# Dilated attention in a two-stream encoder: both heads of a pair side by side, queries and keys stored block by block

## Chip, core and metric

The kernel runs on one core of a Trainium2 chip. The metric is the device time of one execution in microseconds. The five engines that the text names are PE (TensorE, with PEld for its weight loads), DVE (VectorE), ACT (ScalarE), POOL (GpSimd) and SP (which issues transfers).

## What is computed

Two independent sequences ("streams") of 512 tokens and width 1024 pass through a trunk of two layers with shared weights. Layer 0 mixes tokens by dilated window attention and a Hyena convolution, layer 1 by a bidirectional RWKV recurrence; each is followed by a convolutional feed-forward part. The change is in the attention of layer 0. There are three groups of four heads of width 64, with (window, dilation) = (128, 1), (512, 4), (2048, 16):

```python
s = jnp.einsum('bnqhd,bnkhd->bhnqk', qc, kw) * (Dh ** -0.5)   # q, k: the tokens of one residue class
s = jnp.where(valid, s + alibi, NEG_INF)                      # alibi: -slope * |distance|
m = jnp.max(s, axis=-1, keepdims=True)
p = jnp.exp(s - m)
den = jnp.sum(p, axis=-1, keepdims=True)
o = jnp.einsum('bnhqk,bnkhd->bnqhd', p / den, vw)
```

The outputs of the three groups are then merged per head, weighted by their denominators.

## The kernel before

Activations lie transposed, channels on the partitions and 512 tokens in the free dimension. A dense product (`dense`, L124) loads a weight tile (tile `wraw`, a transfer issued by ACT), splits it into a high part on ACT (`whi`, L108) and a low part on POOL (`wlo`, L112), and makes 24 matmuls of FP32R into a PSUM tile `pd`, of which there are three. An evacuation function then copies `pd` out.

Work is written as Python generators that yield their estimated cost. `weave` (L84) and `run` (L1283) interleave them by these estimates, and a scheduler under the program then sets each engine's order. In the first stage the attention of stream 0 is interleaved with `ada_params` (L192), which streams 48 weight tiles `adaw` of 1 MB through three buffers and multiplies each in four matmuls of 32 columns. Stream 1's attention runs later, between the feed-forward matmuls of stream 0.

The attention (L447) goes through six parts (g, hp): group g of three, head pair hp of two. While one part attends, the next is projected. A projection makes `V` (the value columns of the group's four heads, for hp = 0; PSUM tiles `pv`) and two tiles `qk0` and `qk1` of 128 x 512: queries and keys of the two heads of the pair, one head in each half of the partitions (rows 0 to 63 and 64 to 127). In groups 1 and 2 the 512 tokens are four blocks of 128 tokens with equal index modulo 4. `perm(ap, g, b)` picks block b with a stride of four tokens; for V it is applied to the stationary operand.

`attend` (L484) takes one head of the pair after the other. For group 0 each of four blocks has its own score tile of 256 or 384 keys. For groups 1 and 2 the four blocks of 128 queries by 128 keys share one score tile. DVE adds the masked ALiBi term into an SBUF tile `sb` and takes the maximum into `nm` (L503, L504, L514, L516). `attend_blocks` (L525) makes the exponential on ACT (L527), transposes on PE (`self.tr`), copies the result into `pt` on ACT or DVE (L536, L534), and multiplies it with `V` into the half of the partitions of the tile `ops` that belongs to the head. All score tiles, transpositions, `ops` and the accumulator of `ada_params` are PSUM tiles `ps` from one pool of five buffers per stream (L671). At the end ACT copies `ops` to `O`, reordering the tokens of groups 1 and 2 (L521).

After both streams' attention, `combine` (L545) multiplies in the merging weights; its matmuls with `e` (tiles `cme`) have 64 columns and alternate between the halves of the partitions of their output. In the RWKV loop, the matmuls of `X` with `AR` (lines 1193 to 1195) alternate in the same way between the halves of their input partitions.

Of the kernel before, what the change touches and what calls it, by code (L numbers as in the profile page):

```python
# [17 lines left out]
L = 512  # L18
# [33 lines left out]
class K:  # L52
# [387 lines left out]
    def attention(self, s, hs, ap, op, then, early):  # L440
# [11 lines left out]
        def project(g, hp):  # L452
# [18 lines left out]
            for i, m in enumerate((g * 2 + hp, 6 + g * 2 + hp)):  # L471
                t = ap.tile([128, L], F32, tag=f"qk{i}", bufs=2, name=f"qk{i}")
                qk[g, hp].append(t)
                yield from self.dense(a["win"][m], KC, xs, lambda ps: nc.scalar.activation(t, ps, AF.Copy, scale=0.125 if i == 0 else 1.0))

        parts = [(g, hp) for g in range(3) for hp in range(2)]
        yield from project(*parts[0])
# [7 lines left out]
    def attend(self, ap, g, hp, qk, V, rel, nm, den, O, op):  # L485
        nc = self.nc
        ops = self.ps()
        last = None
        for h in range(2):
            row = slice(h * 64, h * 64 + 64)  # L490
            head = hp * 2 + h
            slope = -(2.0 ** (-8.0 * (g * 4 + head + 1) / 12))
            q, k = (t[row] for t in qk)
            blocks = []
            if g == 0:
                for b in range(4):
                    k0, k1 = max(0, b - 1), min(3, b + 1) + 1
                    w = (k1 - k0) * 128
                    ps = self.ps()
                    self.mm(ps[:, :w], q[:, b * 128:b * 128 + 128], k[:, k0 * 128:k1 * 128], start=True, stop=True)  # L500
                    sb = ap.tile([128, 512], F32, tag="sb", bufs=3, name="sb")
                    o = 128 if b == 0 else 0
                    nc.vector.scalar_tensor_tensor(sb[:, :w], rel[:, o:o + w], slope, ps[:, :w], ALU.mult, ALU.add)  # L503
                    nc.vector.tensor_reduce(nm[:, g, b, head:head + 1], sb[:, :w], AX.X, ALU.max, negate=True)  # L504
                    blocks = [(b, sb[:, :w], [(kb, (kb - k0) * 128) for kb in range(k0, k1)])]
                    last = self.attend_blocks(ap, g, head, row, blocks, V, nm, den, ops, last)
                    yield 860 + 600
            else:
                ps = self.ps()
                for b in range(4):  # L510
                    self.mm(ps[:, b * 128:b * 128 + 128], self.perm(q, g, b), self.perm(k, g, b), start=True, stop=True)
                sb = ap.tile([128, 512], F32, tag="sb", bufs=3, name="sb")
                s3 = sb.rearrange("p (b k) -> p b k", b=4)
                nc.vector.scalar_tensor_tensor(s3, rel[:, None, 256 + 128 * g:384 + 128 * g].to_broadcast([128, 4, 128]), slope,  # L514
                                               ps.rearrange("p (b k) -> p b k", b=4), ALU.mult, ALU.add)
                nc.vector.tensor_reduce(nm[:, g, :, head], s3, AX.X, ALU.max, negate=True)  # L516
                blocks = [(b, s3[:, b], [(b, 0)]) for b in range(4)]
                last = self.attend_blocks(ap, g, head, row, blocks, V, nm, den, ops, last)
                yield 4 * (218 + 110 + 218)
        t = op.tile([128, L], F32, tag=f"O{g}{hp}", name="O")  # L520
        nc.scalar.copy(self.unperm(t, g), self.unperm_src(ops, g))  # L521
        O[g, hp] = t

    def attend_blocks(self, ap, g, head, row, blocks, V, nm, den, ops, last):
        nc = self.nc  # L525
        for b, p, keys in blocks:
            nc.scalar.activation(p, p, AF.Exp, bias=nm[:, g, b, head:head + 1], accum_out=den[:, g, b, head:head + 1])  # L527
            tp = self.ps()
            w = len(keys) * 128
            for kb, o in keys:  # L530
                self.tr(tp[:, o:o + 128], p[:, o:o + 128], self.ident)
            pt = ap.tile([128, 384], F32, tag="pt", bufs=2, name="pt")
            if b % 2:
                nc.vector.tensor_copy(pt[:, :w], tp[:, :w])  # L534
            else:
                nc.scalar.copy(pt[:, :w], tp[:, :w])  # L536
            for n, (kb, o) in enumerate(keys):
                mm = self.mm(ops[row, b * 128:b * 128 + 128], V[:, kb, head * 64:head * 64 + 64], pt[:, o:o + 128],
                                      start=n == 0, stop=n == len(keys) - 1)
                if n == 0 and last is not None:  # L540
                    self.after(mm, last)
            last = mm
        return last

    def combine(self, s, ap, nd, z, O, out):  # L545

# [36 lines left out]
    def hyena_in(self, s, hs, pool, tmp):  # L583
# [5 lines left out]
        for part, c in ((1, 0), (1, 1), (2, 0), (2, 1), (0, 0), (0, 1)):  # L589
            i = part * 2 + c  # L590

            def evac(ps):
                if part == 2:
                    t = tmp.tile([128, L], F32, tag="sb", bufs=3, name="hv")
                else:
                    t = (x0 if part == 0 else z)[c]
                self.dwconv(t, ps, lambda j: self.v("sw", j * 6 + i), self.v("sb", i))
                if part == 2:
                    nc.gpsimd.tensor_tensor(z[c], z[c], t, ALU.mult)
# [885 lines left out]
```

## Time and profile before

| | us |
|---|---|
| median of the three runs shown | 3595.82 (3590.41 to 3604.41) |
| the profiled execution | 3581.8 |
| its span, first to last instruction | 3580.0 |
| PE busy | 3311.5 (92%) |
| DVE, ACT, POOL busy | 1707.0, 1576.7, 1603.4 |
| first scores of stream 0 / last products of stream 0 begin | 133.04 / about 377 |
| first scores / last products of stream 1 | about 501 / about 849 |

A row of the timeline has the start, the time from the first start to the last end, the engine, the line, the operation, the tiles (written<-read), for PE the part of the array (rows*columns) and the shape of the output, and xN for N records merged. Helper functions record the matmuls, so all of them stand on L78 and all transpositions on L81; they are told apart by their tiles. In brackets stands the idle time of the engine ahead, and what ended it.

### The profile page before, as it was taken

The numbers are of one execution on the slowest core, as the hardware profiler recorded it, in microseconds if no ns is written. First come the engines' busy times: TensorE is split into PE (matmuls) and PEld (weight loads), VectorE is DVE, ScalarE is ACT, GpSimd is POOL, SyncE is SP. The second block draws the span as 40 slices with busy tenths as digits, with TensorE's granted clock in tenths as the row PEclk, the third lists the DMA queues.
The fourth block names the chain that finished last, engine by engine and source line by source line (L and its number), as shares of the span: only waits on it lengthen the run. The fifth ranks groups of instructions, "written<-read, shape, count | busy, mean of one in ns | idle before, by whom it ended". The sixth has DMA issues, their size and how long they took to land. (4 is left out here: it accounts for less than half of the span.)

```text
span 3580.0 us, 62660 instructions
## 1 busy us (share of the span) xinstructions
PE 3311.5 (92%) x24082; PEld 2367.3 (66%) x24082; DVE 1707.0 (48%) x3181; ACT 1576.7 (44%) x3139; POOL 1603.4 (45%) x1480
## 2 busy tenths in 40 slices
PE   7999989999999899999998897798999999989998
PEld 4555767887877676676665564466666666667776
DVE  5021442212335555386677658467677663442223
ACT  3122244434334445545556557444555454443332
POOL 2111342334435665464444557455445443444443
PEclk9999999999999999999998997798999999999999
DMA  7655141222344224654445441574444443342322
GB/s 247 227 188 192 59 136 54 76 71 86 127 132 143 97 95 165 218 155 113 115 126 135 130 121 49 198 250 152 114 113 118 127 106 94 123 159 91 97 89 88
DMA packets 378787, 463.26 MB, mean 129 GB/s; under 512 B 201239, under 2 KB 218903, under 8 KB 377080
## 3 DMA queue, kind: packets, MB, share of 16 engines
q1 hardware_dynamic: 302928, 247.78, 22.7%
q10 hardware_dynamic: 75560, 211.48, 18.6%
q8 instruction: 189, 3.10, 0.4%
q14 instruction: 110, 0.90, 0.1%
HBM read 378.11 MB, written 81.00 MB: 128 GB/s over the span
## 5 line engine op out<-in xcount | busy, mean ns | idle before, releaser
L112 POOL TENSOR_TENSOR wlo<-wraw,whi 128x512 fp32r<-128x512 f32 (+1 forms) x830 | 1086.2, 1313 | 1356.4 <-ACT whi L108 1184.7
L108 ACT CAST whi<-wraw 128x512 fp32r<-128x512 f32 (+1 forms) x830 | 497.5, 606 | 877.3 <-PE pd L78 675.8
L78 PE MATMUL pd<-midh,whi 128*128 128x512 f32 x704 | 287.9, 410 | 6.2 <-ACT midh L141 6.2
L78 PE MATMUL pd<-midl,whi 128*128 128x512 f32 x704 | 282.9, 402 | 0.9 <-DVE midl L144 0.3
L78 PE MATMUL pd<-midh,wlo 128*128 128x512 f32 x704 | 282.4, 402 | 0.3 <-POOL wlo L112 0.3
L328 DVE SCALAR_TENSOR_TENSOR x<-pd,ada,x 128x512 f32<-128x512 f32 x192 | 142.7, 746 | 196.0 <-PE pd L78 195.2
L78 PE MATMUL pd<-xml,whi 128*128 128x512 f32 (+1 forms) x448 | 191.1, 427 | 21.2 <-DVE xml L144 13.7
L78 PE MATMUL pd<-xmh,whi 128*128 128x512 f32 (+1 forms) x448 | 195.4, 438 | 5.5 <-ACT xmh L141 5.4
L78 PE MATMUL pd<-xmh,wlo 128*128 128x512 f32 (+1 forms) x448 | 186.8, 418 | 3.9 <-POOL wlo L112 3.7
L1226 POOL TENSOR_TENSOR Sg<-S,G 128x256 f32<-128x256 f32 x144 | 102.9, 714 | 169.5 <-DVE S L1224 156.2
L291 DVE SCALAR_TENSOR_TENSOR fa<-pd,vecs,fa 128x511 f32<-128x511 f32 x88 | 65.7, 746 | 231.9 <-ACT fa L290 231.9
L1211 ACT COPY UV<-X 32x128 f32<-32x128 f32 x512 | 131.6, 257 | 93.4 <-PE X L78 65.7
L321 DVE TENSOR_TENSOR fa<-fa,pd 128x512 f32<-128x512 f32 x88 | 60.4, 686 | 214.0 <-PE pd L78 202.3
L78 PEld LDWEIGHTS pd<-midh,whi 128*128 128x128 f32 x704 | 132.7, 189 | 40.6 <-ACT midh L141 9.2
L78 PEld LDWEIGHTS pd<-midl,whi 128*128 128x128 f32 x704 | 133.3, 189 | 33.4 <-DVE midl L144 4.2
L78 PEld LDWEIGHTS pd<-midh,wlo 128*128 128x128 f32 x704 | 132.9, 189 | 31.1 <-POOL wlo L112 0.7
L1224 DVE TENSOR_TENSOR S<-X,Sg 128x256 f32<-128x256 f32 x144 | 60.6, 421 | 185.1 <-ACT ys L1222 181.8
L78 PE MATMUL X<-UV,Am 32*32 32x64 f32 (+1 forms) x4096 | 127.5, 228 | 20.3 <-ACT UV L1211 17.4
L1141 DVE TENSOR_TENSOR W<-W,sub 128x120 f32<-128x120 f32 (+7 forms) x496 | 136.3, 275 | 11.1
L78 PEld LDWEIGHTS X<-UV,Am 32*32 32x32 f32 (+1 forms) x4096 | 79.0, 108 | 86.2 <-ACT UV L1211 64.3
L1139 DVE TENSOR_TENSOR sub<-U,W 128x120 f32<-128x120 f32 (+7 forms) x496 | 128.8, 260 | 14.7 <-DMA U<-inv 3.9
L78 PEld LDWEIGHTS pd<-xml,whi 128*128 128x128 f32 (+1 forms) x448 | 88.5, 198 | 53.4 <-DVE xml L144 26.2
(477 smaller groups left out, 8007.0 us busy)
## 6 DMA issues: line engine op xcount, KB each, us to landing
wraw<-in_up ACTq DMA_DIRECT2D x176, 512.0 KB, 3.5
adaw<-in_adaw SPq DMA_DIRECT2D x96, 512.0 KB, 5.2
wraw<-in_dn ACTq DMA_DIRECT2D x128, 256.0 KB, 2.7
wraw<-in_win ACTq DMA_DIRECT2D x36, 512.0 KB, 3.5
x<-x SPq DMA_DIRECT2D x48, 256.0 KB, 3.4
wraw<-in_dn ACTq DMA_DIRECT2D x64, 192.0 KB, 2.4
x<-res SPq DMA_DIRECT2D x32, 256.0 KB, 3.0
wraw<-in_wk ACTq DMA_DIRECT2D x16, 512.0 KB, 3.6
```

Source lines behind the costliest of these rows:

```text
L78: return self.nc.tensor.matmul(*a, **k)
L108: nc.scalar.copy(h, raw[:, o:o + w])
L112: nc.gpsimd.tensor_tensor(l, raw[:, o + p:o + p + w2], h[:, p:p + w2].bitcast(F32), ALU.subtract)
L291: nc.vector.scalar_tensor_tensor(t[:, 1:], ps[:, :L - 1], w(0), t[:, 1:], ALU.mult, ALU.add)
L321: nc.vector.tensor_tensor(act, act, ps, ALU.mult)
L328: nc.vector.scalar_tensor_tensor(x[m], ps, self.ada[l][:, 40 + m, s:s + 1], x[m], ALU.mult, ALU.add)
L1139: nc.vector.tensor_tensor(w, U4[:, :, k:, e * K + k:e * K + k + 1].to_broadcast(shape), W4[:, e:e + 1, k:k + 1, 0:k + 1].to_broadcast(shap ...
L1141: nc.vector.tensor_tensor(W4[:, :, k:, 0:k + 1], W4[:, :, k:, 0:k + 1], w, ALU.add)
L1211: nc.scalar.copy(dst, X[ur, :, uu(g)])
L1224: nc.vector.tensor_tensor(S, X[:, :, 384:512].rearrange("p d (g v) -> p d g v", g=2), self.Sg, ALU.add)
L1226: nc.gpsimd.tensor_tensor(Sg, S, self.G[:, tau, :, :, None].to_broadcast([128, 2, 2, 64]), ALU.mult)
```

## The change

The change is all in layer 0's attention.

- The evacuation of `qk0` and `qk1` now reads `pd` with the stride and writes `qk` in the order of the blocks, so that the score matmuls read contiguous columns. It did a plain copy with a scale before.
- `attend` makes the scores of both heads of the pair, head inside block, into two PSUM tiles, then the masks and maxima of both.
- `attend_block` replaces `attend_blocks` and takes one block of both heads: exponential, transposition and copy of head 0, then of head 1 (ACT copies head 0, DVE head 1; before, ACT copied even blocks, DVE odd ones), then the products, alternating between the heads.
- `sb` has four buffers instead of three, `pt` four instead of two. The estimated costs that the generators yield are split anew, in groups 1 and 2 also lower.

```diff
-                yield from self.dense(a["win"][m], KC, xs, lambda ps: nc.scalar.activation(t, ps, AF.Copy, scale=0.125 if i == 0 else 1.0))
+                yield from self.dense(a["win"][m], KC, xs, lambda ps: nc.scalar.activation(self.unperm_src(t, g), self.unperm(ps, g), AF.Copy, scale=0.125 if i == 0 else 1.0))
...
-        for h in range(2):
-            row = slice(h * 64, h * 64 + 64)
...
+                ps = [self.ps() for _ in range(2)]
+                for h in range(2):
+                    self.mm(ps[h][:, :w], q[rows[h], b * 128:b * 128 + 128], k[rows[h], k0 * 128:k1 * 128], start=True, stop=True)
+                sb = [ap.tile([128, 512], F32, tag="sb", bufs=4, name="sb") for _ in range(2)]
...
-                    self.mm(ps[:, b * 128:b * 128 + 128], self.perm(q, g, b), self.perm(k, g, b), start=True, stop=True)
...
+            ps = [self.ps() for _ in range(2)]
+            for b in range(4):
+                for h in range(2):
+                    self.mm(ps[h][:, b * 128:b * 128 + 128], q[rows[h], b * 128:b * 128 + 128], k[rows[h], b * 128:b * 128 + 128], start=True, stop=True)
...
+            yield 4 * (218 + 110)
+            for b in range(4):
+                last = self.attend_block(ap, g, hp, b, [t[:, b] for t in s3], [(b, 0)], V, nm, den, ops, last)
+                yield 2 * 110 + 2 * 218
...
+    def attend_block(self, ap, g, hp, b, p, keys, V, nm, den, ops, last):
...
+        for h in range(2):
+            head = hp * 2 + h
+            nc.scalar.activation(p[h], p[h], AF.Exp, bias=nm[:, g, b, head:head + 1], accum_out=den[:, g, b, head:head + 1])
+            tp = self.ps()
             for kb, o in keys:
-                self.tr(tp[:, o:o + 128], p[:, o:o + 128], self.ident)
-            pt = ap.tile([128, 384], F32, tag="pt", bufs=2, name="pt")
-            if b % 2:
...
+                self.tr(tp[:, o:o + 128], p[h][:, o:o + 128], self.ident)
+            pt.append(ap.tile([128, 384], F32, tag="pt", bufs=4, name="pt"))
+            if h:
...
+        for n, (kb, o) in enumerate(keys):
+            for h in range(2):
+                head = hp * 2 + h
+                mm = self.mm(ops[h * 64:h * 64 + 64, b * 128:b * 128 + 128], V[:, kb, head * 64:head * 64 + 64], pt[h][:, o:o + 128],
+                             start=n == 0, stop=n == len(keys) - 1, skip_group_check=True)
```

The change also moves instructions. A first place is on PE in stream 0, at the scores of the second dilated part (g = 1, hp = 1); `pv<-whi` and `pv<-wlo` are the value projection of the next group, `adaw` the modulation weights, `pt,V` the products, `ident,sb` the transpositions. Before, for head 0 and later for head 1 (a gap of some 25 rows between the two pieces):

```order
L78 MATMUL ps<-pt,V 64x128 x2
L78 MATMUL ps<-adaw,sc 32x512 x2
L78 MATMUL ps<-qk_1567,qk_1432 128x128 x2
L78 MATMUL ps<-pt,V 64x128
L78 MATMUL ps<-qk_1567,qk_1432 128x128 x2
L78 MATMUL pv<-whi,h5l 128x256
...
L78 MATMUL ps<-adaw,sc 32x512
L78 MATMUL ps<-qk_1567,qk_1432 128x128
L78 MATMUL ps<-adaw,sc 32x512 x2
L78 MATMUL ps<-qk_1567,qk_1432 128x128 x3
L78 MATMUL pv<-wlo,h6h 128x256
```

Now:

```order
L78 MATMUL pv<-wlo,h3h 128x256
L78 MATMUL ps<-adaw,sc 32x512 x8
L78 MATMUL ps<-qk_1567,qk_1432 128x128 x8
L78 MATMUL ps<-adaw,sc 32x512 x6
L78 MATMUL pv<-whi,h4h 128x256
```

The eight score matmuls of the part, in four runs before, stand together, head 0 and head 1 in turn; the products that stood between are gone, and the matmuls with `adaw` gather on both sides of them.

The second place is on PE a little later in the same part, at its transpositions and products. Before (head 0):

```order
L78 MATMUL ps<-pt,V 64x128
L81 MATMUL ps<-ident,sb 128x128
L78 MATMUL pv<-wlo,h7h 128x256
L81 MATMUL ps<-ident,sb 128x128
L78 MATMUL pv<-whi,h6h 128x256
L78 MATMUL pv<-whi,h6l 128x256
L78 MATMUL ps<-pt,V 64x128
L81 MATMUL ps<-ident,sb 128x128
L78 MATMUL ps<-adaw,sc 32x512
L78 MATMUL ps<-pt,V 64x128 x2
```

Now (both heads):

```order
L78 MATMUL ps<-pt,V 64x128
L81 MATMUL ps<-ident,sb 128x128
L78 MATMUL ps<-pt,V 64x128
L81 MATMUL ps<-ident,sb 128x128
L78 MATMUL pv<-wlo,h5h 128x256
L78 MATMUL pv<-whi,h4h 128x256
L81 MATMUL ps<-ident,sb 128x128
L78 MATMUL ps<-pt,V 64x128 x2
L78 MATMUL pv<-whi,h4l 128x256
```

The two heads' products of a block, one key block each here, stand next to each other only in some places; elsewhere a transposition or dense matmuls lie between them.

## Rows read from the trace of the kernel before

**Rows 1.** The page: busy time by engine.
```profile
PE 3311.5 (92%) x24082; PEld 2367.3 (66%) x24082; DVE 1707.0 (48%) x3181; ACT 1576.7 (44%) x3139; POOL 1603.4 (45%) x1480
```

**Rows 2.** Windows: stretch, length, busy PE, PEld, DVE, ACT, POOL, clock, DMA share, GB/s.
```profile
130.00:377.00 247.00, 246.40 (x1015) 141.78 (x1015) 41.78 (x94) 65.60 (x176) 36.71 (x29) 1.00 0.51 182
501.00:849.00 348.00, 342.04 (x1465) 268.83 (x1465) 87.76 (x141) 150.10 (x294) 119.51 (x93) 0.99 0.21 67
```

**Rows 3.** Waits of PE (us, times, longest): longest row of 130:377, then of 501:849.
```profile
PE ps L78 <- DMA adaw<-in_adaw: 0.6, 1, 0.6
...
PE ps L81 <- ACT sb L527: 4.1, 3, 2.2
```

**Rows 4.** Timeline of PE: dilated scores, and what follows each run.
```profile
286.73 0.83 PE L78 MATMUL ps<-qk,qk 64*128 64x128 f32 x2
287.49 1.05 PE L78 MATMUL ps<-adaw,sc 128*32 128x512 f32 x4
288.47 1.77 PE L78 MATMUL ps<-qk,qk 64*128 64x128 f32 x6
290.17 0.51 PE L78 MATMUL pv<-wlo,h6h 128*128 128x256 f32 x1
```

**Rows 5.** The same timeline: undilated scores of 256 and 384 keys, and what follows.
```profile
133.04 0.70 PE L78 MATMUL ps<-qk,qk 64*128 64x256 f32 x2
133.66 0.51 PE L78 MATMUL pv<-whi,h2l 128*128 128x256 f32 x1
...
143.42 0.91 PE L78 MATMUL ps<-qk,qk 64*128 64x384 f32 x2
144.26 0.51 PE L78 MATMUL pv<-wlo,h5h 128*128 128x256 f32 x1
```

**Rows 6.** The same timeline: products of one head, two (before 143.42) and three matmuls.
```profile
142.84 0.65 PE L78 MATMUL ps<-pt,V 128*64 128x128 f32 x4
...
150.56 0.87 PE L78 MATMUL ps<-pt,V 128*64 128x128 f32 x6
151.36 1.05 PE L78 MATMUL ps<-adaw,sc 128*32 128x512 f32 x4
```

**Rows 7.** The same timeline: matmuls on alternating halves of the array.
```profile
408.84 2.84 PE L78 MATMUL ps<-ident,cme 128*64 128x128 f32 x48
411.61 1.99 PE L78 MATMUL ps<-zt,dc 128*128 128x256 f32 x8
...
1625.97 0.34 PE L78 MATMUL X<-S,AR 64*64 64x64 f32 x8
1626.24 0.41 PE L78 MATMUL X<-UV,Am 32*32 32x64 f32 x8
```

**Rows 8.** The same timeline: four matmuls with adaw, and one.
```profile
264.89 1.06 PE L78 MATMUL ps<-adaw,sc 128*32 128x512 f32 x8
...
285.76 1.05 PE L78 MATMUL ps<-adaw,sc 128*32 128x512 f32 x2
```

**Rows 9.** The same timeline: dense matmuls after and ahead of another tile shape.
```profile
290.51 0.40 PE L78 MATMUL pv<-whi,h7h 128*128 128x256 f32 x1
290.74 0.40 PE L78 MATMUL pv<-whi,h7l 128*128 128x256 f32 x1
...
291.68 0.40 PE L78 MATMUL pv<-wlo,h6h 128*128 128x256 f32 x1
292.00 1.05 PE L78 MATMUL ps<-adaw,sc 128*32 128x512 f32 x4
```

**Rows 10.** ACT's copy O (min/median/max ns); the loads of adaw in 130:377 (us to landing).
```profile
L521 ACT COPY O<-ps x12: 586/1072/1097, 195.1 to 848.8; 128x512 f32<-128x512 f32 x12
...
adaw<-in_adaw SPq DMA_DIRECT2D x58, 512.0 KB, 5.1
```

**Rows 11.** Timeline: a transposition and its copy.
```profile
268.37 0.27 PE L81 MATMUL ps<-ident,sb 128*128 128x128 f32 x1
268.68 0.27 ACT L536 COPY pt<-ps 128x128 f32<-128x128 f32 x1 [0.89 <-PE ps L81]
```

More of the change, by code (lines that the diff above doesn't have):

```diff
@@ L488, in attend @@
         last = None
-        for h in range(2):
-            row = slice(h * 64, h * 64 + 64)
[L491 to L510, printed above, removed]
-                    self.mm(ps[:, b * 128:b * 128 + 128], self.perm(q, g, b), self.perm(k, g, b), start=True, stop=True)
[L512 to L519, printed above, removed]
@@ L522, in attend @@
         O[g, hp] = t
-    def attend_blocks(self, ap, g, head, row, blocks, V, nm, den, ops, last):
+    def attend_block(self, ap, g, hp, b, p, keys, V, nm, den, ops, last):
         nc = self.nc
-        for b, p, keys in blocks:
-            nc.scalar.activation(p, p, AF.Exp, bias=nm[:, g, b, head:head + 1], accum_out=den[:, g, b, head:head + 1])
+        w = len(keys) * 128
+        pt = []
+        for h in range(2):
+            head = hp * 2 + h
+            nc.scalar.activation(p[h], p[h], AF.Exp, bias=nm[:, g, b, head:head + 1], accum_out=den[:, g, b, head:head + 1])
             tp = self.ps()
-            w = len(keys) * 128
             for kb, o in keys:
-                self.tr(tp[:, o:o + 128], p[:, o:o + 128], self.ident)
-            pt = ap.tile([128, 384], F32, tag="pt", bufs=2, name="pt")
-            if b % 2:
-                nc.vector.tensor_copy(pt[:, :w], tp[:, :w])
-            else:
[L536 to L540, printed above, removed]
+                self.tr(tp[:, o:o + 128], p[h][:, o:o + 128], self.ident)
+            pt.append(ap.tile([128, 384], F32, tag="pt", bufs=4, name="pt"))
+            if h:
+                nc.vector.tensor_copy(pt[h][:, :w], tp[:, :w])
+            else:
+                nc.scalar.copy(pt[h][:, :w], tp[:, :w])
+        for n, (kb, o) in enumerate(keys):
+            for h in range(2):
+                head = hp * 2 + h
+                mm = self.mm(ops[h * 64:h * 64 + 64, b * 128:b * 128 + 128], V[:, kb, head * 64:head * 64 + 64], pt[h][:, o:o + 128],
+                             start=n == 0, stop=n == len(keys) - 1, skip_group_check=True)
+                if n + h == 0 and last is not None:
                     self.after(mm, last)
-            last = mm
-        return last
+        return mm
     def combine(self, s, ap, nd, z, O, out):
@@ L593, in evac @@
                 if part == 2:
[L594 removed]
+                    t = tmp.tile([128, L], F32, tag="sb", bufs=4, name="hv")
                 else:
```

19 lines of the change are left out of this document (added).

## Prediction, made before the changed kernel ran

> **What bounds the kernel now.** I read the page first: TensorE (PE) is busy 3311.5 of 3580.0 us, no other engine over half [rows 1]. The change touches only the attention of the two streams, so next I cut out that stretch by windows: from 130 us (first scores of the first stream are at 133.04) to 849 us (last products of the second). In the two windows that hold attention, 130 to 377 and 501 to 849 us, PE is busy nearly all the time, DVE, ACT and POOL under half of it, and the granted clock is 1.00 and 0.99 [rows 2]. Busy time alone proves little for PE, so I asked what PE waited for: 0.6 us, a single wait, in the first window, and in the second 4.1 us for exponentials, every other row there being under 1 us [rows 3]. PE's own instruction stream is therefore the bound there, and time taken out of it is time off the end, as long as the waits stay small. Outside the stretch the order of PE's instructions is the same in both programs, so the rest only moves earlier.
>
> **How PE's time is priced.** The shown durations overlap. What an instruction costs is the distance from its start to the next start, and I take a run (neighbours of one kind) from its first start to the start of what follows. Every FP32 matmul shows as two records, a transposition as one.
>
> - Scores of a dilated group (128 keys, one head): a run of one block takes 0.76 us, of three 1.70 (286.73 to 287.49, 288.47 to 290.17) [rows 4]. That is 0.29 for the run and 0.47 per block.
> - Scores of the undilated group: 0.84 us for 384 keys (143.42 to 144.26), 0.62 for 256 (133.04 to 133.66) [rows 5]. 256 contiguous keys cost less than 128 strided ones. The part per key is 0.21 per 128 keys, which leaves 0.20 for the run.
> - Products of one head: 0.58 us for two matmuls (142.84 to 143.42), 0.80 for three [rows 5, 6]: 0.22 each, 0.15 for the run.
> - Two heads side by side: the combine step has the products' very shape (128*64, 128x128), alternating between the heads' column halves. Its 24 matmuls (x48) take 408.84 to 411.61, 2.77 us [rows 7]; less 0.15, that is 0.22 per pair. The second head is free. For two row halves, which scores need, the nearest row is X<-S,AR, neighbours of which read opposite halves and write different halves of the PSUM tile X (lines 1193 to 1195): eight records in 0.27 us, the run's fixed part included [rows 7]. Eight single passes of half the products' columns would alone need 8 x 0.055 = 0.44.
> - The ada matmuls (128*32) have the same property: one, two or four of them (x2, x4, x8) show the same 1.05 or 1.06 us, and one takes 285.76 to 286.73, two 287.49 to 288.47 [rows 4, 8]. I count 0.98 us per slot of up to four.
> - A change to another tile shape also costs the dense work: the first dense matmul after it takes 0.34 instead of 0.23 us, the last before it 0.32 (290.17 to 290.51, 290.51 to 290.74, 291.68 to 292.00) [rows 4, 9]. That is 0.20 per excursion.
>
> **The change, part by part.** The counts come from the two orders, between the first score and the last product, both streams together. PE's instructions of each kind are the same in number; their grouping and their stride differ.
>
> 1. Dilated scores: 64 matmuls, in 25 runs before and 11 after, stride gone. Before: 25 x 0.29 + 64 x 0.47 = 37.3 us. After, neighbours of opposite heads share a slot, which leaves 34 slots at 0.22: 11 x 0.20 + 34 x 0.22 = 9.7. Gain 27.6.
> 2. Undilated scores: 16 matmuls of each width, each a run of its own: 16 x 0.62 + 16 x 0.84 = 23.4. After, 7 of 8 narrow pairs and 4 of 8 wide pairs stand together, so 9 and 12 runs of one slot: 15.7. Gain 7.7.
> 3. Products: 144 matmuls in 85 runs: 85 x 0.15 + 144 x 0.22 = 44.4. After, 76 runs with 101 slots (in the dilated groups the two heads are mostly still parted by a transposition or dense work): 33.6. Gain 10.8.
> 4. Ada matmuls, moved along by the new order: 126 in 67 slots, 65.7 us; after, in 55 slots, 53.9. Gain 11.8.
> 5. Excursions from the dense work: 155 before, 123 after: 32 x 0.20 = 6.4.
>
> Sum of the gains: 64.3 us. At the start of the second dilated part of the first stream, the first order place shows terms 1 and 4 at once; the second place shows why term 3 is small.
>
> Against it:
>
> - The strided access moves to the eviction of the 16 dilated projections on ACT. ACT's copy O takes 0.59 us in group 0, without a stride, and 1.07 as the median of all groups, most of them strided [rows 10]. Its stride is on the output side; the trace has no strided read of PSUM at this size, so the price is bounded by 0 and 0.5 us each, 8 us of ACT in all. ACT is busy 27% and 43% of the two windows [rows 2] and PE has three banks to go on with, so I take 0 and keep 8 for the range. Queued behind it on ACT stand exponentials and weight casts.
> - A product still waits for a transposition to be copied out: 0.31 us until the copy starts, 0.27 for it [rows 11], so 0.6 to 0.7 before a product can follow. In the old order 2 products have less than 0.7 us of PE work (at the prices above) between them and their transposition, in the new one 12. At 0.2 us each that is 2 us more.
> - Between scores and the first transposition DVE and ACT have mask, maximum and exponential to do, now for two heads in a row. The new order has 2.7 us of PE work or more in between in all but two cases, the old one in all but two as well; I take nothing.
> - One burst of ada matmuls now wants a fourth tile of three buffers some 3 us after the first is released, while a load takes 5.1 us to land [rows 10]: 3 us. DMA is busy for 0.51 of the first window [rows 2]; a stretch shorter by a seventh asks for 0.59.
> - I add 3 us for waits of the kind that PE has now.
>
> Sum of the costs: 8 us, with 0 and 25 as ends. Net 56.
>
> [...] The trace's pairs in the combine step share all rows and differ in columns, and cost 0.22 us a pair [rows 7]. [...] In the trace of before the longest row of PE's waits is for an exponential, not for a copy that frees a bank [rows 3].
>
> **The rivals.**
>
> - Pairs don't overlap. Scores of two row halves with 128 columns each stand nowhere in the trace, and the products of two heads, whose weights share all rows, may pair less well than the combine step's. Then term 1 has 64 slots (30 x 0.22 = 6.6 lost), term 2 loses 7 x 0.42 + 4 x 0.64 = 5.5, term 3 loses 43 x 0.22 = 9.4. With the products alone the gain is 56 - 9 = 47, a time of 3549; with all three it is 56 - 21.5 = 35, a time of 3561. For it: no row of this exact shape. Against it: [rows 7]. Chance 0.13, of which 0.03 for the products alone.
> - The chain becomes the bound in part. PE runs faster, the chain from scores over DVE and ACT to products doesn't. If half of the 48 blocks expose one copy round (0.6 us) and each of the 8 dilated parts 1.4 us for the second head, that is 26 us on top: with one of the two alone as the other end the gain is 30 to 45, the time 3551 to 3566. For it: PE did wait 4.1 us for exponentials already [rows 3]. Against it: the work that stands between. Chance 0.16.
> - Slower, through PSUM banks. The pool has 5 buffers (L671). The accumulating product holds one, ada in the first stream another, two scores two; one is left for transpositions. If each block then runs transposition, copy, transposition, copy with nothing under it, 1.3 us are bare per block, 62 us over 48 blocks, which eats the gain; from 1.75 us a block on (the waits for both score buffers added) the kernel is over 18 us slower: 48 x 1.75 - 64.3 = 19.7, time 3615. Against it: the new order lays dense work between in most blocks. Chance 0.05, of which 0.03 slower.
> - The change doesn't do what it says: the score step might not be due to the stride. Then the slots of term 1 stay at 0.47 each and the gain falls by 34 x 0.25 = 8.5. The 256-key row speaks against it; it lies inside the range.
>
> **How the numbers follow.** The profiled execution took 3581.8 us (span 3580.0); the sum makes that 3526. The median of the runs shown is 3595.82, 14 above the profiled one; I put the gain on the median: 3595.8 - 56 = 3540. My forecast (gain 45 to 72) gets 0.66, the rivals 0.13, 0.16 and 0.05. The range for eight in ten goes from 3519 (no costs, and some us of scatter: the runs shown span 14) to 3572 (the far end of the two partial rivals, 3566, and the same scatter). About 0.5%, 18 us, is what a measurement of this kernel tells from no change; faster by more gets 0.92, same 0.05, slower 0.03.
>
> **What would show it.** In the changed trace: dilated scores as runs of x16 of some 1.1 us (0.20 + 4 x 0.22) instead of x2 to x8 with 0.47 a block (term 1); products of undilated blocks as one run after both transpositions (term 3); fewer and longer ada runs (term 4); qk evictions between 0.6 and 1.1 us; PE's waits for sb and pt under 15 us in the stretch; and the last products of the second stream at about 849 - 56 = 793 us, with the rest of the span as long as now. I am wrong if a x16 run takes near 2 us (no pairing), or if PE's waits for ACT or DVE in the stretch reach 25 us.

## The result, and the profile after

The changed kernel took 3542.53 us (median of four runs, 3517.01 to 3549.78), the kernel before 3593.36 beside it. The ratio is 0.9837, with a 95% interval from 0.9806 to 0.9867: 1.3 to 1.9% faster. The prediction was 3540 us, with a range from 3519 to 3572.

The profiled execution took 3541.3 us, its span is 3539.5. First the busy times on the page of after, which answer to [rows 1]:

```profile
PE 3260.7 (92%) x24082; PEld 2336.5 (66%) x24082; DVE 1710.2 (48%) x3181; ACT 1573.0 (44%) x3137; POOL 1601.0 (45%) x1480
```

PE has the same 24082 matmul records and is busy 50.8 us less; DVE, ACT and POOL are busy as before to within 4 us. The work on PE is the same, it is only packed better. Next the two windows that hold attention, which answer to [rows 2] with the same columns (stretch, length, busy PE, PEld, DVE, ACT, POOL, clock, DMA share, GB/s):

```profile
130.00:347.00 217.00, 212.07 (x1000) 121.61 (x1000) 41.22 (x92) 63.27 (x173) 35.17 (x28) 0.98 0.56 202
473.00:788.00 315.00, 308.53 (x1449) 244.39 (x1449) 85.31 (x141) 145.24 (x289) 117.12 (x91) 0.99 0.23 72
```

They are 30 and 33 us shorter (247 to 217, 348 to 315), and PE is still busy 98% of each. PE's waits there (us, times, longest), the two longest rows of 130:347 and then of 472:789, answer to [rows 3]:

```profile
PE ps L78 <- DMA adaw<-in_adaw: 4.7, 3, 3.2
PE ps L81 <- ACT sb L534: 0.2, 1, 0.2
...
PE ps L81 <- ACT sb L534: 5.1, 5, 2.5
PE pv L78 <- POOL wlo L112: 0.6, 1, 0.6
```

The waits for exponentials (`sb`) are 5.3 us in all, 4.1 before. The row that grew is the first one, for the `adaw` loads: 4.7 us, 0.6 before. The last products of the second stream on PE's timeline:

```profile
787.70 0.43 PE L78 MATMUL ps<-pt,V 128*64 128x128 f32 x2
788.07 0.50 PE L78 MATMUL pd<-h3h,whi 128*128 128x512 f32 x1
```

From the first scores (131.73) to what follows the last products (788.07) the stretch is 656.3 us; it was 715.6 (133.04 to 848.7). That is 59.3 us less, while the span of the two profiled executions fell by 40.5 only. The rest of the text takes these two numbers apart.

**The single steps on PE's timeline.** Undilated scores of both heads, 256 keys, then what follows; against [rows 5]:

```profile
131.73 0.70 PE L78 MATMUL ps<-qk,qk 64*128 64x256 f32 x4
132.37 1.05 PE L78 MATMUL ps<-adaw,sc 128*32 128x512 f32 x4
```

Two heads in 0.64 us, where one took 0.62. Dilated scores of a whole part, against [rows 4]:

```profile
335.86 1.16 PE L78 MATMUL ps<-qk,qk 64*128 64x128 f32 x16
336.95 0.50 PE L78 MATMUL pd<-h0h,whi 128*128 128x512 f32 x1
```

Eight matmuls of four blocks and two heads in 1.09 us. The prediction had named 1.1, from 0.20 for the run and 4 x 0.22. Before, one head of three blocks took 1.70. Products, first an undilated block, then the dilated place that the prediction spoke of; against [rows 6]:

```profile
152.94 0.87 PE L78 MATMUL ps<-pt,V 128*64 128x128 f32 x10
153.74 1.05 PE L78 MATMUL ps<-adaw,sc 128*32 128x512 f32 x4
...
241.72 0.27 PE L81 MATMUL ps<-ident,sb 128*128 128x128 f32 x1
241.92 0.43 PE L78 MATMUL ps<-pt,V 128*64 128x128 f32 x2
242.29 0.44 PE L81 MATMUL ps<-ident,sb 128*128 128x128 f32 x2
242.65 0.43 PE L78 MATMUL ps<-pt,V 128*64 128x128 f32 x2
```

Five matmuls of two heads take 0.80 us, as three of one head did. In the dilated part the products still stand alone between transpositions, each 0.37 us to the next start.

The eviction of `qk` on ACT (minimum, median and maximum in ns of 24), with the strided read of PSUM, and the copy `O`, which answers to [rows 10]:

```profile
L474 ACT ACTIVATE qk<-pd x24: 586/592/603, 90.2 to 754.2; 128x512 f32<-128x512 f32 x24
...
L524 ACT COPY O<-ps x12: 585/1068/1105, 182.5 to 788.6; 128x512 f32<-128x512 f32 x12
```

The same row of the kernel before, where the eviction had no stride:

```profile
L474 ACT ACTIVATE qk<-pd x24: 572/593/634, 91.5 to 803.5; 128x512 f32<-128x512 f32 x24
```

### The profile page after: what moved, and what is told of

Read it like the earlier page. It is cut to its first block, busy times and chain, and to the rows that moved or that the text cites. A ratio compares the mean times of both kernels' runs of the same rounds, so it can differ in the third digit from the quotient of the medians.

```text
span 3539.5 us, 62668 instructions
## 1 busy us (share of the span) xinstructions
PE 3260.7 (92%) x24082; PEld 2336.5 (66%) x24082; DVE 1710.2 (48%) x3181; ACT 1573.0 (44%) x3137; POOL 1601.0 (45%) x1480
## 5 line engine op out<-in xcount | busy, mean ns | idle before, releaser
L78 PEld LDWEIGHTS pd<-midh,whi 128*128 128x128 f32 x704 | 133.6, 190 | 42.4 <-ACT midh L141 10.2
```

Source lines behind the costliest of these rows:

```text
L78: return self.nc.tensor.matmul(*a, **k)
```

## The experiments

The table has PE's time in the attention stretch by kind of matmul, from the start of a run to the start of what follows, added up over the trace; "dense" is the matmuls into `pd` and `pv`, "tail" what comes after the last product. All in us; e1 to e9 (there is no e5) are described below. Not in the table are the transpositions (20.4 us before, 20.0 after) and the other matmuls into `ps` (36.7 and 37.8). A wait of PE is counted with the run ahead of it: of the 4.7 us for `adaw` in the trace of after, 3.2 stand under dense and 1.5 under ada.

| kernel | stretch | undilated scores | dilated scores | products (runs) | ada (runs) | dense | tail |
|---|---|---|---|---|---|---|---|
| before | 715.6 | 25.7 | 37.3 | 44.2 (85) | 65.8 (67) | 485.7 | 2731.3 |
| before, again | 715.8 | 25.7 | 37.3 | 44.4 (85) | 65.8 (67) | 485.2 | 2743.1 |
| after | 656.3 | 18.5 | 11.3 | 34.2 (76) | 58.2 (52) | 476.3 | 2751.4 |
| after, again | 654.1 | 18.5 | 10.1 | 34.2 (76) | 55.4 (52) | 477.9 | 2746.2 |
| after, third | 653.8 | 18.5 | 10.6 | 34.4 (76) | 56.1 (52) | 476.2 | 2748.7 |
| e1 block order only | 697.0 | 25.7 | 20.1 | 44.5 (85) | 65.8 (67) | 483.5 | 2745.4 |
| e2 side by side only | 662.7 | 18.5 | 19.2 | 34.5 (76) | 55.1 (52) | 479.3 | 2744.5 |
| e2, again | 662.3 | 18.5 | 19.2 | 34.5 (76) | 55.1 (52) | 478.6 | 2747.3 |
| e3 scores in turn | 657.8 | 18.5 | 15.8 | 32.8 (72) | 58.3 (53) | 474.0 | 2737.9 |
| e4 products in turn | 662.5 | 19.8 | 10.8 | 39.0 (77) | 57.4 (53) | 477.5 | 2747.3 |
| e6 four PSUM buffers | 657.1 | 18.4 | 11.0 | 33.6 (76) | 59.7 (55) | 477.2 | 2736.1 |
| e7 dilated blocks gathered | 642.8 | 18.5 | 10.8 | 27.2 (45) | 55.9 (52) | 475.9 | 2738.3 |
| e8 queries strided | 708.3 | 25.7 | 34.7 | 43.7 (85) | 65.8 (67) | 481.4 | 2744.3 |
| e9 keys strided | 710.7 | 25.7 | 33.6 | 44.4 (85) | 65.8 (67) | 483.8 | 2752.7 |

### The two halves of the change, each alone

Block order only: the kernel before with the new eviction and contiguous score matmuls. Every engine's order stays that of the kernel before.

```diff
-... lambda ps: nc.scalar.activation(t, ps, AF.Copy, ...)
+... lambda ps: nc.scalar.activation(self.unperm_src(t, g), self.unperm(ps, g), AF.Copy, ...)
-self.mm(ps[:, b * 128:b * 128 + 128], self.perm(q, g, b), self.perm(k, g, b), start=True, stop=True)
+self.mm(ps[:, b * 128:b * 128 + 128], q[:, b * 128:b * 128 + 128], k[:, b * 128:b * 128 + 128], start=True, stop=True)
```

> The kernel before with one edit: the projections' evacuation writes queries and keys in the order of their blocks, and the score matmuls read them without a stride. Heads stay one after the other; PE's order is that of before, row by row. My theory (the stride costs PE time by itself): the 64 dilated scores go from 37.3 us (25 x 0.29 + 64 x 0.47) to 19.1 (25 x 0.20 + 64 x 0.22), 18 us less, everything else as before; first score to last product 715.6 - 18 = 698 us; the run 18 us shorter than before. Rival 'the stride is not the cause': dilated scores stay at 37 us and the time stays. Rival 'strided evacuation costs ACT': qk evacuations rise from 0.59 towards 1.07 us and PE's waits rise by up to 8 us.

Measured: 3572.22 us, ratio to before 0.9934 (0.9912 to 0.9956), and a stretch of 697.0, 18.6 less than before. The dilated scores fell from 37.3 to 20.1. Two of their runs (x4, from 698.87) lie at the lower clock and take 1.15 us instead of 0.64; without that they would be at the 19.1 expected. A run of four blocks of one head, and what follows it, in its timeline:

```profile
342.46 1.16 PE L78 MATMUL ps<-qk,qk 64*128 64x128 f32 x8
343.54 0.50 PE L78 MATMUL pd<-h6h,wlo 128*128 128x512 f32 x1
```

The same run in the kernel before:

```profile
348.14 2.24 PE L78 MATMUL ps<-qk,qk 64*128 64x128 f32 x8
350.31 0.50 PE L78 MATMUL pd<-h6h,wlo 128*128 128x512 f32 x1
```

2.17 us became 1.08. With the stride as the only difference in this run, it shows that the stride was half the price of a dilated score; the stretch falls by about what the scores fall (18.6 and 17.2 us), so the strided eviction takes nothing back.

Side by side only: the changed kernel with the old storage. Every engine's order stays that of the changed kernel.

```diff
-... lambda ps: nc.scalar.activation(self.unperm_src(t, g), self.unperm(ps, g), AF.Copy, ...)
+... lambda ps: nc.scalar.activation(t, ps, AF.Copy, ...)
-self.mm(ps[h][:, b * 128:b * 128 + 128], q[rows[h], b * 128:b * 128 + 128], k[rows[h], b * 128:b * 128 + 128], ...)
+self.mm(ps[h][:, b * 128:b * 128 + 128], self.perm(q[rows[h]], g, b), self.perm(k[rows[h]], g, b), ...)
```

> The changed kernel with the stride put back: plain evacuation, strided reads in the scores; both heads side by side, PE's order that of the changed kernel, row by row. My theory: everything but the stride's part stays gained, that is 7 (undilated scores) + 10 (products) + 8 (ada) + 6 (excursions) = 31 us; the strided dilated scores in pairs are new: 34 slots x 0.47 + 11 x 0.29 = 19 us if two strided weight loads in opposite row halves share a slot, 64 x 0.47 + 11 x 0.29 = 33 if not. So the run is 49 us or 35 us shorter than before. Rival 'the gain is the stride alone': the run is near before.

Measured: 3539.88 us, ratio 0.9841 (0.9804 to 0.9878), stretch 662.7, that is 52.9 less than before. The run of eight strided matmuls, two heads:

```profile
336.13 2.25 PE L78 MATMUL ps<-qk,qk 64*128 64x128 f32 x16
338.30 0.50 PE L78 MATMUL pd<-h0h,whi 128*128 128x512 f32 x1
```

It takes 2.17 us, exactly what the four of one head took before: strided matmuls pair as well as contiguous ones do. The 52.9 us are a little more than the 49 expected for this case. By the times alone this kernel can't be told from the changed one (0.9841 against 0.9837); its stretch and its dilated scores tell them apart. So the halves overlap. Alone they bring 18.6 and 52.9 us, together 59.3 to 61.8 (the three traces of after): side by side halves the number of slots that the stride makes dear, and the block order is then worth 6 to 9 us instead of 18.6.

### Which of the two strides costs

The score matmul has the queries as its stationary operand (the weight load) and the keys as the moving one. The kernel of block order only, with one of the two stored and read as in the kernel before again; every engine's order is that of the kernel before. Queries strided:

```diff
-self.mm(ps[...], q[:, b * 128:b * 128 + 128], k[:, b * 128:b * 128 + 128], start=True, stop=True)
+self.mm(ps[...], self.perm(q, g, b), k[:, b * 128:b * 128 + 128], start=True, stop=True)
```

> The kernel before with the keys stored block by block, the queries as before and read with the stride. The queries are the stationary operand of the score matmul, the keys the moving one; PE's order is that of the kernel before, row by row. Measured so far: dilated scores 37.3 us with both strided, 20.1 with neither. Theory (the stride costs in the weight load): nearly the whole price stays, dilated scores 35 to 38 us, attention stretch about 714. Rival (it costs in the moving operand): 20 us, stretch about 698. If it is split evenly: about 29 us.

Measured: 34.7 us for the dilated scores. The time was 3586.97 us in one run, 3594.43 for the kernel before beside it.

```profile
346.70 2.13 PE L78 MATMUL ps<-qk,qk 64*128 64x128 f32 x8
348.76 0.50 PE L78 MATMUL pd<-h6h,wlo 128*128 128x512 f32 x1
```

Keys strided:

```diff
-self.mm(ps[...], q[:, b * 128:b * 128 + 128], k[:, b * 128:b * 128 + 128], start=True, stop=True)
+self.mm(ps[...], q[:, b * 128:b * 128 + 128], self.perm(k, g, b), start=True, stop=True)
```

> The same with the queries stored block by block and the keys read with the stride. Theory (weight load): dilated scores 20 us, attention stretch about 697. Rival (moving operand): 35 to 38 us, stretch about 714.

Measured: 33.6 us. The time was 3596.95 us in one run beside the same 3594.43; single times that scatter by more than 10 us say nothing about 3 us.

```profile
346.66 2.06 PE L78 MATMUL ps<-qk,qk 64*128 64x128 f32 x8
348.64 0.50 PE L78 MATMUL pd<-h6h,wlo 128*128 128x512 f32 x1
```

My theory (it is the weight load) and its rival (it is the moving operand) both fall, and so does an even split. Either stride alone costs nearly the whole: the run takes 1.08 us with none, 2.06 with the queries', 1.98 with the keys', 2.17 with both. Between two passes inside a run the starts lie 112, 234, 227 and 235 ns apart. So the price is not a sum but the larger of two. The reading that fits: load and matmul run beside each other, and whichever reads with the stride sets the pace. The weight loads of the same runs go with it: each starts before the matmul ahead of it has ended, and takes 0.19 us with neither stride and 0.33 with the queries'. A change that had stored only the keys, or only the queries, by blocks would have gained 2.6 or 3.7 us instead of 17.2 (the lower clock adds nothing, 0.2 and 1.0 us to the scores of e8, e9 and e1).

### The pairs

Dilated scores, one head after the other:

```diff
-            for b in range(4):
-                for h in range(2):
+            for h in range(2):
+                for b in range(4):
                     self.mm(ps[h][:, b * 128:b * 128 + 128], q[rows[h], ...], k[rows[h], ...], start=True, stop=True)
```

> The changed kernel with the dilated scores of head 0 first, all four blocks, then those of head 1: the stride stays gone, but neighbours now use the same half of the rows. My theory (opposite row halves share a slot): slots go from 34 to 57, so the dilated scores take 57 x 0.22 + 11 x 0.20 = 14.7 us instead of the 11.3 measured (9.7 by the same prices): 5 us more; a run of x16 takes 1.5 to 2 us instead of 1.09. First score to last product 5 us longer. Rival 'row halves don't pair, the 1.09 us has another cause': no change in the x16 runs.

Measured: 3530.38 us in one run; dilated scores 15.8 us, 4.5 more than after.

```profile
337.94 1.71 PE L78 MATMUL ps<-qk,qk 64*128 64x128 f32 x16
339.58 0.50 PE L78 MATMUL pd<-h0h,whi 128*128 128x512 f32 x1
```

1.64 us instead of 1.09: the pairs are worth 0.55 a run. Eight slots of 0.22 and 0.20 for the run would be 1.96; where head 0 ends and head 1 begins, three starts still follow the one before them by 4 to 6 ns, so some of the two heads' passes pair across the border. That settles the pairs, run against run. The stretch was to be 5 us longer and is 1.5 (657.8): with this edit the scheduler also orders PE anew (72 runs of products instead of 76), and products and dense work come out 1.4 and 2.3 us shorter. The single time is below that of after because the tail of this trace is 13.5 us shorter, within the scatter of tails shown below.

Products, one head after the other:

```diff
-        for n, (kb, o) in enumerate(keys):
-            for h in range(2):
+        for h in range(2):
+            for n, (kb, o) in enumerate(keys):
```

> The changed kernel with the products of a block made for head 0 first, then for head 1. My theory (opposite column halves share a slot): slots go from 101 to 125, so the products take 24 x 0.22 = 5 us more than the 34.2 us measured; first score to last product 5 to 7 us longer. Rival 'column halves that share all rows don't pair in products': no change in the products' time per run.

Measured: 3543.6 us in one run; products 39.0 us, 4.8 more, stretch 662.5.

```profile
152.22 0.87 PE L78 MATMUL ps<-pt,V 128*64 128x128 f32 x6
153.02 0.91 PE L78 MATMUL ps<-qk,qk 64*128 64x384 f32 x2
153.86 0.87 PE L78 MATMUL ps<-pt,V 128*64 128x128 f32 x6
154.66 1.05 PE L78 MATMUL ps<-adaw,sc 128*32 128x512 f32 x4
```

Three matmuls of one head take 0.80 us here, and five of both heads take the same 0.80 in after (152.94). Two heads whose weights share all rows and differ in columns do overlap; in the run at 152.94 their weight loads start in pairs, 6 to 8 ns apart, while matmuls run. So the rival that pairs don't overlap falls for the products too.

### The suspected costs

PSUM: the pool of the score and transposition tiles with four buffers instead of five, in the changed kernel.

```diff
-            self.psm[s] = self.pool(f"psm0{s}", bufs=5, space=PSUM, ctx=c3, side=side)
+            self.psm[s] = self.pool(f"psm0{s}", bufs=4, space=PSUM, ctx=c3, side=side)
```

> The changed kernel with four instead of five PSUM buffers in the attention's pool. My theory (dense work in PE's order covers the attention's waits, banks are not the limit): PE's waits in the attention rise by under 10 us, first score to last product stays within 10 us of 656. Rival 'the pairs live at the edge of the PSUM pool': one bank less bares a copy round (1.3 us) for most of the 48 blocks, 30 to 60 us more.

Measured: 3537.13 us, ratio to before 0.9846 (0.9819 to 0.9873), stretch 657.1. The longest waits of PE from 130 to 850 us:

```profile
PE ps L81 <- ACT sb L534: 5.3, 6, 2.5
PE pv L78 <- DVE res L283: 4.3, 1, 4.3
PE ps L78 <- DMA adaw<-in_adaw: 3.7, 2, 3.1
```

No wait for a copy that frees a buffer is among them, and none of the three is longer than in after (5.3, 4.3 and 4.7). Even a buffer fewer is enough, so the rival "slower, through PSUM banks" falls.

Products parted by transpositions: in the dilated parts, make all exponentials and transpositions of a head first, one copy for the four blocks, and then all eight products.

```diff
             yield 4 * (218 + 110)
+            pt = []
+            for h in range(2):
+                head = hp * 2 + h
+                tp = self.ps()
+                for b in range(4):
+                    nc.scalar.activation(s3[h][:, b], s3[h][:, b], AF.Exp, bias=nm[:, g, b, head:head + 1], accum_out=den[:, g, b, head:head + 1])
+                    self.tr(tp[:, b * 128:b * 128 + 128], s3[h][:, b], self.ident)
+                pt.append(ap.tile([128, 512], F32, tag="pw", bufs=2, name="pw"))
...
             for b in range(4):
-                last = self.attend_block(ap, g, hp, b, [t[:, b] for t in s3], [(b, 0)], V, nm, den, ops, last)
-                yield 2 * 110 + 2 * 218
+                for h in range(2):
+                    ...
+                    mm = self.mm(ops[h * 64:h * 64 + 64, b * 128:b * 128 + 128], V[:, b, head * 64:head * 64 + 64], pt[h][:, b * 128:b * 128 + 128], ...)
```

> A version that goes on from the changed kernel: in the dilated groups the four transpositions of a head go into one PSUM tile, one copy of 512 columns takes them out, and the eight products of the pair follow each other, heads in turn. My theory (runs and excursions cost 0.15 and 0.20 us, pairs are free): products in 45 runs and 93 slots instead of 76 and 101, 4.7 + 1.8 us less; excursions from dense work 93 instead of 123, 6 us less; 12 us in all, first score to last product 644 us, the run about 12 us shorter than the changed kernel. Rival 'the chain becomes the bound': the products wait for all exponentials of a head, PE's waits for the copies rise by 12 us or more and nothing is gained.

Measured: 3523.59 us (3514.48 to 3537.26, six runs), ratio 0.9816 (0.9790 to 0.9843), stretch 642.8. The run of products that the prediction missed in the dilated parts of the changed kernel is there:

```profile
246.37 1.09 PE L78 MATMUL ps<-pw,V 128*64 128x128 f32 x14
247.39 0.51 PE L78 MATMUL pv<-whi,h1l 128*128 128x256 f32 x1
```

Seven matmuls, four slots, in 1.02 us. Products fall from 34.2 to 27.2 us in 45 runs instead of 76, transpositions from 20.0 to 16.6. PE waits 1.0 us for the new copies (`pw`), so the rival of the chain falls here too. But the sum that foretold it is only half right: 6 of its 12 us were to come from fewer breaks in the dense work (places where scores, transpositions, products or ada matmuls stand between matmuls into `pd` and `pv`), and the dense row did not move (475.9). Counted in the traces there are 156 breaks, 146 in after, since transpositions now stand alone more often. The stretch is 11 to 13.5 us shorter than in the traces of after, and the median 13.5 us below that of the kernel with four buffers, which was timed beside it and has the stretch of after. The intervals of the two ratios overlap, so by the times alone it is not settled; by the stretch, whose traces repeat within 2.5 us, it is the faster version.

### What the span lost behind the attention

The changed kernel a second and third time, and the kernel before a second time:

> The changed kernel once more, for a second trace. Between first score and last product 656 us, as in the first. After the last product the first trace took 20 us more than the kernel before, though PE's order there is the same. My theory: that is the granted clock, which spent 318 us at its lower level after the attention against 292 before, and it differs from run to run: this trace will show another figure, and the time after the last product moves with it by about half. Rival 'the change itself costs time later, by what it shifts': again about 318 us low and about 2751 us from the last product to the end.

> The kernel before once more, for a second trace. First score to last product 716 us. My theory: the time at the lower clock after the attention differs from the first trace's 292 us, and the time from the last product to the end from 2731 us, by about half as much. Rival: both are as in the first trace, which would make the 20 us a cost of the change.

> The changed kernel a third time. The stage of some 200 us that holds stream 1's RWKV projection took 208.0 and 206.9 us in the two traces of it so far, with 44 us at the lower clock, and 197 to 200 us with 15 to 19 in the kernel before and in most variants, on the same order of PE. If the program (its timing) decides this: again 206 to 209 us and 44 to 48 at the lower clock. If it is chance from run to run: either. Attention stretch 654 to 657 us by both.

> The kernel with the heads side by side and the strided storage of before, again; its first trace had 199.5 us and 17 at the lower clock in that stage, on the very order of the changed kernel. If the program decides: again 197 to 200 us; if chance: either. Attention stretch 662 to 664 us, dilated scores 19.2.

Measured: after again 3531.28 us (ratio 0.9812, 0.9777 to 0.9847), before again 3593.25 (0.9992, 0.9972 to 1.0012), after a third time 3543.63 and side by side a second time 3545.5, the last two in one run each. The stretches repeat within 2.5 us, the tails do not: 2731.3 and 2743.1 in one and the same kernel before.

The largest part that moves is a stage of some 200 us with stream 1's RWKV projection. Its windows in the two traces of side by side, from and to the same instructions of DVE:

```profile
1293.00:1492.50 199.50, 185.94 (x723) 127.72 (x722) 95.80 (x120) 97.89 (x159) 105.07 (x89) 0.96 0.58 193
```

```profile
1293.20:1504.50 211.30, 197.56 (x720) 138.08 (x720) 96.06 (x122) 98.22 (x159) 103.09 (x90) 0.89 0.55 182
```

One program, the stage entered at the same time to 0.2 us, and yet 199.5 us at a granted clock of 0.96 and 211.3 at 0.89. In the second the clock is at its lower level for 6.8 us every 20.5 us, from 1375.0 on; in the first it falls four times in all, at no regular distance. I had expected that the program might decide this, since after, after again, e3 and e4 all showed 206 to 209 us and before, e1, e6 and e7 197 to 199. It does not decide it alone: side by side showed both, and keys strided, in the order of the kernel before, 213.2. But the changed kernel showed 208.0 a third time, in three traces of three, and the kernel before 197 and 199 in its two. That the change makes the longer course more likely is not excluded. What starts the series stays open. The expectations above tied the tail to the time at the lower clock. That held for before again (12 us more at the lower clock after the attention, a tail 11.8 longer) and not for after again (7.7 more, a tail 5.2 shorter), so a sum of that time alone does not tell the tail.

The five traces in the order of the kernel before (before twice, e1, e8, e9) have a mean tail of 2743.4 us, the five in the order of after (after three times, e2 twice) 2747.6. Of the 4.2 us between them 3.3 is work that changed sides: 14 of the dense matmuls, at 0.236 us each, now come after the last product instead of before it. What is left is far inside the scatter of single tails (2731 to 2753), so no run shows a cost of the change there, and none of a few us could be seen.

## Why the prediction was right, step by step

The last column takes out PE's waits, and half of the time at the lower clock (0.50 granted, in the window under step 4), as an estimate of what that clock costs the dense and ada work; step 1 is taken from after again, where no score run lies at that clock. For the dense row the estimate can be tried: so treated it is 465.3 to 465.9 us in the five traces in the order of before and 457.6 to 458.2 in the five in the order of after, where the table has 481.4 to 485.7 and 476.2 to 479.3.

| step | foretold gain | measured (before less after) | without waits and lower clock |
|---|---|---|---|
| 1 dilated scores | 27.6 | 26.0 (27.2 and 26.7 in the other traces) | 27.5 |
| 2 undilated scores | 7.7 | 7.2 | 7.5 |
| 3 products | 10.8 | 10.0 | 10.0 |
| 4 ada matmuls | 11.8 | 7.6 | 10.8 |
| 5 excursions | 6.4 | 6.1 (dense work 9.4 less, of which 3.3 moved out) | 3.9 (7.2 less 3.3) |
| sum | 64.3 | 56.9 | 59.7 |
| costs | 8 | in the rows above | 3.8 (waits) |

- **Bound.** PE's own stream set the end, as said: 59.3 us less of it in the stretch is 59.3 us less time there. Less the 3.3 us that only moved, 56.0 are left, and the net of the sum was 56. The last products begin at 787.70, foretold at about 793. That the net agrees so closely is partly luck: the gains are some 5 us smaller than the sum had them and the costs some 4 us smaller (PE's waits in the stretch rose by 3.8 us, from 15.4 to 19.2, where 8 were put). The other two traces of after have a net of 58.
- **Price of a slot.** The prices taken from the combine step and from X<-S,AR [rows 7] held: 1.09 us for the run of x16, 0.80 for five products in three slots, 1.02 for seven in four. Both kinds of pairs had been borrowed from other steps of the kernel, of other tiles or other sizes.
- **Step 1** is short by 1.6 us in the first trace. After PE had stood still for the `adaw` load, the clock was at its lower level (0.50 in the window below), and two of the score runs lie there, a x6 at 232.24 with 1.15 us and a x10 at 235.24 with 1.58. At the usual price, in after again, they are 0.64 and 0.86. The other two traces have 10.1 and 10.6, near the 9.7 foretold; in the third the x6 lies at the lower clock too.
- **Step 4 and the ada burst.** The count of slots was nearly right: without waits and lower clock the ada matmuls take 55.0 us, foretold 53.9. The burst that wants a fourth tile of three buffers (14 `adaw` matmuls, three and a half tiles, around the scores of the second dilated part) does wait, but 0.72 us and not the 3 foretold: its load lands 3.6 us after it is issued (259.29), not 5.1.

```profile
261.10 1.07 PE L78 MATMUL ps<-adaw,sc 128*32 128x512 f32 x8
262.89 1.05 PE L78 MATMUL ps<-adaw,sc 128*32 128x512 f32 x4 [0.72 <-DMA adaw<-in_adaw]
```

  The long wait, 3.20 us, stands elsewhere, and the sum did not have it. It only happens to have the size foretold for the burst:

```profile
222.92 0.60 PE L81 MATMUL ps<-ident,adam 128*128 128x128 f32 x4
...
226.79 0.40 PE L78 MATMUL pd<-h3h,wlo 128*128 128x512 f32 x1
230.39 1.92 PE L78 MATMUL ps<-adaw,sc 128*32 128x512 f32 x4 [3.20 <-DMA adaw<-in_adaw]
232.24 1.22 PE L78 MATMUL ps<-qk,qk 64*128 64x128 f32 x6
```

```profile
230.30:236.90 6.60, 6.51 (x25) 2.77 (x25) 0.39 (x1) 0.00 (x0) 0.00 (x0) 0.50 0.92 335
```

  At 222.92 one group of modulation columns is finished, and only then are the first loads of the next group issued (223.59). In the kernel before, PE came to the next group's first `adaw` matmul 8.1 us after that transposition (239.86 to 247.94) and did not wait; in the denser order it is ready after 4.3 us, while the load takes 6.7 to land. The last row is a window on the time behind the wait: the granted clock was 0.50 for 6.6 us, so two runs of ada matmuls took 1.85 us each instead of 0.98. The sum had nothing for that either. In the third trace of after the clock was low for 3.4 us behind it, in the second not at all; their stretches are 2.5 and 2.2 us shorter, about what this cost the first.
- **Eviction.** Taken at nothing, with 8 us kept for the range. It is nothing: 592 ns with the strided read of PSUM, 593 without. The stride costs ACT where it writes (`O`, 1068 against 585).
- **Step 5** is where the sum was most off, 3.9 us for 6.4. The 6.1 of the table is that by chance: the trace of before has 15.2 us of dense work at the lower clock and that of after 6.9, worth some 4 us, and the waits under dense are 2.0 us longer in after (the 3.20 among them). Counted in the traces, the breaks in the dense work fell from 173 to 146, by 27 and not by 32; the price of 0.20 also came from single rows, and the mean over the breaks of a trace is 0.18.
- **Chain.** PE's waits for exponentials went from 4.1 to 5.3 us, and no wait for `pt` is in either window, together under the 15 that were to show it right. The rival of the chain falls.
- **The stride.** That it might not be the cause, the rival inside the range, falls with block order only. But the prediction had one price for "strided" and no word on which operand it belongs to. Both strides have to go, which this change did.
- **The rest of the span** was not "as long as now" in the first trace: 20.1 us longer. This step of the prediction was too narrow. 3.3 us moved there. The rest lies within the scatter of the fourteen tails: the trace of before happens to have the shortest of all, that of after the second longest (e9 has the longest), and one stage alone moves by 12 us in one and the same program. The median stands beside it: 50.8 us less in the first comparison, 63.3 in the second (3594.55 to 3531.28), around the 56 foretold.

## What to carry to other kernels

Where matmuls use half the array, put neighbours on opposite halves next to each other: the second one was free here, for row halves (four blocks take 1.08 us for one head and 1.09 for two, with a stride 2.17 for either) and for column halves (0.80 us for three products of one head and for five of two). Where the new order brings other small matmuls together, as the ada matmuls here (65.8 us to 55.4 in after again), they gain too; but look at what they wait for, since a denser order comes to its loads sooner (after 4.3 us instead of 8.1 here). Take a stride out of both operands of a matmul or expect little (2.6 or 3.7 us here for one alone, 17.2 for both), and move it to a read of PSUM by ACT, where it cost nothing here (592 ns against 593). Price such a change by runs and slots taken from other steps of the same trace, and compare the stretch that is changed before the span, since the rest of this span scatters by 20 us. Do not take a net that agrees for terms that agree: here two misses of 4 to 5 us cancelled.

## What was not expected of the hardware

- A read of SBUF with this stride of four FP32 values halves the pace of either operand of these FP32 matmuls, and two strides cost no more than one: 112 ns between passes with none, 234, 227 and 235 with the queries', the keys' and both. ACT's strided read of PSUM, 592 ns against 593, shows none of it.
- The lower clock hardly touches what the stride has made slow: two contiguous blocks take 1.15 us at the lower clock and 0.64 at the higher (e1, 698.87 and 260.02), two blocks with strided keys 1.19 and 1.08 (e9, 708.40 and 260.56).
- At the wait of 3.2 us for `adaw` the clock fell to its lower level for 6.8 us (from 230.0) in one of three traces of the changed kernel; it was 3.4 us in another and nothing in the third, with waits of 3.1 and 3.0 there. The six other traces with the heads side by side have 3.4 to 10.2.
- In the projection stage the lower clock comes back every 20.5 us in some executions (side by side again, from 1375.0) and not in others (side by side the first time), with PE's order the same, for 12 us in 200 (211.3 against 199.5).
